# Five small edits to a decoder-layer kernel: gate products in exact parts, a token-major first query block, a root carried in the last sum, squares moved, and four raw weight tiles in another pool

## The chip, the cores and the metric

One core of a Trainium2 chip runs the whole layer in one launch. The metric is the device time of an execution in microseconds; lower is better. Profiles are of one execution each, and their span is somewhat shorter than the device time.

## The reference, cut to what matters

A decoder layer in float32 for one sequence of 256 tokens and width 2048:

```python
hn = rmsnorm(h, norm_mix_w)
q, k, v, g_ret, xr, yr, g_a, g_b = split(hn @ w_in)            # 2048 -> 14336 columns
ret_out = silu(g_ret) * head_groupnorm(chunkwise_retention(rotary(q), rotary(k), v))
xr = causal_dwconv(xr)                                          # 4 taps
gate_r = sigmoid(blockdiag(xr, rg_w_a) + b_a)                   # 16 blocks of 128x128
gate_i = sigmoid(blockdiag(xr, rg_w_x) + b_x)
a = exp(-8 * gate_r * softplus(-lam))
hr = scan(h = a * h + sqrt(1 - a*a) * gate_i * xr)              # over the tokens
rnn_out = gelu(yr) * hr
h = h + (sigmoid(g_a) * (ret_out @ w_proj_ret) + sigmoid(g_b) * (rnn_out @ w_proj_rnn)) @ w_mix_out
h = h + memory_cross_attention(rmsnorm(h), rmsnorm(mem)) @ xa_w_o   # 4 heads of 512, 256 memory tokens
h = h + (silu(gate) * value) @ ffn_w_down                       # gate, value = conv3(rmsnorm(h) @ ffn_w_up)
return rmsnorm(h, final_norm_w)
```

## The kernel before, in words

**Exact parts.** Every large product is made of three TensorE products of `fp32r` parts: a value is split into `hi`, its rounding to `fp32r`, and `lo`, the rest. Products are hi x hi, lo x hi and hi x lo. Only the gates of the recurrence use plain float32 products (`sm<-xr,rgw`, line 214 through `recur`).

**Weights.** All weights come from one packed array in the order of use, in chunks of 512 rows by 512 columns (1 MB; the first chunks are smaller). For each chunk SyncE (SP) issues the load into a `raw` tile (three buffers), ScalarE (ACT) casts `raw` to `hi` (line 276) and VectorE (DVE) subtracts to get `lo` (line 277), both in two halves of 128x1024 with six buffers each, that is, three chunks. A chunk is loaded and split two chunks ahead of its use (`AHEAD`). The first chunk's `hi` casts are done by DVE (line 274).

**A block** is a product of 256 tokens with a matrix of 512 columns: four chunks of 24 TensorE products of 128x512 (5.45 us a chunk in the chain of waits). `steps_n` makes it by token (tokens in the output's partitions: `products_n`, for both halves `tt` of the tokens); `steps_t` makes it by feature, for the first query block alone; `joined` adds the two halves of its accumulators. The first two blocks of the stream, q and v, run alternately, chunk by chunk, with the chunk sizes of `EARLY`.

**Rows to features.** A block by token that is needed by feature is copied to `rows` (lines 407, 409), its 16-bit halves spread to planes `pl` by two ACT copies (line 385), turned by two DMA transposes that SP issues (`pt<-pl`, line 387), and joined to `f` by two ACT copies (line 396) some chunks later.

**Order.** TensorE's products keep program order (`mm`). What belongs between the chunks is queued by `later(n, fn)` and emitted n + 1 chunks later; the other engines' order is then chosen by a scheduler by priority, and each engine's queue runs in that order. Tiles of 4 KB a partition come from one pool of 27 buffers (`big`), others from pools with few buffers each; a tile that takes a buffer waits for the last reader of what lay there.

**The recurrence** is done in four blocks `b` of 512 features. For each: the XR block and the YR block of `w_in`, then the convolution of XR (lines 775, 777), two bursts (`recur`, `pr` = 0 and 1, emitted `RG_WAIT` and `RG_WAIT + 1` chunks later) of four gate products each, followed by tanh (`tr`, `ti`, lines 742 and 743), exp and tanh (`aa`, `tt`), then root and scan; `gelu_y` makes the stationary parts of the next product.

**The residuals** (`residual`, for w_mix_out and xa_w_o) add a block to `hrow[b]`, square it (line 867) for the next norm, and turn it by `by_dma`. The squares of the memory rows (`memory_steps`) run during the second block of w_mix_out.

**The end.** `last_down` makes the last block of the last product in column halves of 256, with squares and sums for the final norm; `part` collects the earlier sums and `rsqrt_small` (lines 509 to 512) multiplies, adds the epsilon and takes the power -1/2 on GpSimd (POOL).

Of the kernel before, what the change touches and what calls it, by code (L numbers as in the profile page):

```python
# [34 lines left out]
WARM = 8  # L35
URGENT = 5
FREE = 300
# [101 lines left out]
def hybrid_layer(  # L139
# [93 lines left out]
    def prefetch(n):  # L233
        while len(ahead) < n and taken[0] < len(stream):
# [5 lines left out]
            at[0] += size  # L240
            raw = wp.tile([P, KC, BW], F32, tag="raw", bufs=RAW_BUFS, name=nm("raw"))
            k2 = row // (KH * P)
# [5 lines left out]
            for a, b in zip(cuts, cuts[1:]):  # L248
# [62 lines left out]

    def steps_t(w, row, st, nk, col):

        accs = [acc(), acc()]
        first = gemms[0] == 0
        phase = 0
        for k0, n, parts in chunks(nk, w, row, col):
            last = k0 + n >= nk
            tiles = [(kk, j) for j in range(2) for kk in range(n)]
            if first and k0 == 0:  # L320
                runs = [[(t, pr, kk, j) for t in (0, 1)] for kk in range(n) for pr in range(2) for j in range(2)]
            elif last:
                runs = [[(t, pr, kk, j) for kk, j in tiles] for pr in range(2) for t in (1 - pr, pr)]
            else:
                runs = [[(t, pr, kk, j) for pr in range(2) for kk, j in tiles] for t in (phase, 1 - phase)]
                phase = 1 - phase
            for i, run in enumerate(runs):
                for t, pr, kk, j in run:
                    k = k0 + kk
                    sx = st[k // 2][:, k % 2, :]  # L330
                    part = parts[kk // KH][t][:, kk % KH, (2 * pr + j) * P : (2 * pr + j + 1) * P]
                    a = accs[pr][:, j, :]
                    if t == 1:
                        a, sx = a[:, S:BW], sx[:, 0:S]
                    mm(
                        a, part, sx, start=k == 0 and t == 0, stop=k == nk - 1 and t == 0, skip_group_check=True
                    )
                if i + 1 == len(runs) // 2 and not last and not first and isinstance(st, Pairs):
                    st[(k0 + n) // 2 + 1]
            yield accs  # L340

    def gemm_t(*args):
        return ended(steps_t(*args))

    def products_n(o, sx, hi, lo, tt, start, stop):
        h = sx[:, tt * P : (tt + 1) * P]
        l = sx[:, S + tt * P : S + (tt + 1) * P]
        mm(o, h, hi, start=start, stop=False)
        mm(o, l, hi, start=False, stop=False)
        mm(o, h, lo, start=False, stop=stop)  # L350

    def steps_n(w, row, st, nk, col):

        a = acc()
        for k0, n, parts in chunks(nk, w, row, col):
            for tt in range(2):
                for kk in range(n):
                    k = k0 + kk
                    hi, lo = (t[:, kk % KH, :] for t in parts[kk // KH])
                    products_n(a[:, tt, :], st[k // 2][:, k % 2, :], hi, lo, tt, k == 0, k == nk - 1)  # L360
                if tt == 0 and isinstance(st, Pairs):
                    st[min(NT, k0 + 3 * n) // 2 - 1]
            yield a

    def gemm_n(*args):
        return ended(steps_n(*args))
# [34 lines left out]
    def turned_rows(a, r, then, wait=1):  # L401
# [8 lines left out]
        by_dma(rows, then, wait)  # L410

    def joined(a, s="j"):

        c = tmp("c")
        o = tmp(s)
        with tc.high_priority(URGENT):
            act.copy(c, a[:, :, S:BW])
            dve.tensor_tensor(out=o, in0=a[:, :, 0:S], in1=c, op=ALU.add)
        return o

# [161 lines left out]

    qjoin = [joined(t, "q") for t in next(q_steps)]
    assert next(q_steps, None) is None
    later(0, tables)
# [86 lines left out]
    for g in range(2):  # L672
        dec = big([P, 4, S], s="dec")
        vs, turned = [], ([], [])
        for b, o in enumerate((O_Q, O_K)):
            if g + b:
                def rotate_both(f, o=turned[b]):
                    o.append(rotated(f[:, 0:2, :]))
                    later(0, lambda: o.append(rotated(f[:, 2:4, :])))
# [8 lines left out]
            if g + b == 0:  # L688
                turned[0].extend(rotated(q) for q in qjoin)
# [42 lines left out]

    def recur(b, rgw, xr, pr, aa, tt_, ti):

        for j in (2 * pr, 2 * pr + 1):
# [28 lines left out]
    for b in range(4):  # L764
        rgw = big([P, 2, 4, P], s="rgw")
        for i, src in enumerate((rg_w_a, rg_w_x)):
            sp.dma_start(out=rgw[:, i], in_=src[0, 4 * b : 4 * b + 4].rearrange("g i j -> i g j"))
        xr = {}

        def conv_x(f, b=b, xr=xr, rgw=rgw):  # L770
            xr[0] = big([P, 4, S], s="xr")
# [9 lines left out]

            three = []

            def both(pr):
                if pr == 0:
                    three.extend(big([P, 4, S], s=n) for n in ("aa", "tt", "ti"))
                recur(b, rgw, xr[0], pr, *three)

# [51 lines left out]
    def residual(w, st, out, wcol, steps=None):  # L840
# [3 lines left out]
        for b in range(4):  # L844
# [166 lines left out]

    def last_down(b0, hid, n, b):
        h = hrow[b]
        accs = [acc(), acc()]
        parts = [p for _, _, ps in chunks(n, "ffn_w_down", b0 * BW, b * BW) for p in ps]
        for tt in range(2):
            for c in range(2):
                cs = slice(c * S, (c + 1) * S)
                for k in range(n):
                    hi, lo = (t[:, k % KH, cs] for t in parts[k // KH])  # L1020
                    products_n(accs[c][:, tt, 0:S], hid[k // 2][:, k % 2, :], hi, lo, tt, k == 0, k == n - 1)
                y = h[:, tt, cs]
                dve.tensor_add(y, y, accs[c][:, tt, 0:S])
                junk = tp.tile([P, S], F32, tag="tr", bufs=2, name=nm("junk"))
                dve.scalar_tensor_tensor(
                    out=junk, in0=y, scalar=1.0, in1=y, op0=ALU.mult, op1=ALU.mult,
                    accum_out=ss3[:, tt, b + c : b + c + 1],
                )
            part = sp_.tile([P, 1], F32, tag="pt3", bufs=2, name=nm("pt3"))
            dve.tensor_reduce(out=part, in_=ss3[:, tt, 0:4], axis=AX.X, op=ALU.add)  # L1030
            dve.tensor_scalar(out=part, in0=part, scalar1=1.0 / D, scalar2=EPS, op0=ALU.mult, op1=ALU.add)
            r = rsqrt_small(ss3[:, tt, 4:5], 1, 1.0 / D, part)
            for c in (1, 0, 3, 2):
                y = hrow[c][:, tt, :]
                if c == 3:
                    dve.scalar_tensor_tensor(
                        out=y, in0=y, scalar=r, in1=wfin[1][:, 1, :], op0=ALU.mult, op1=ALU.mult
                    )
# [69 lines left out]
```

## Time and profile before

| | us |
|---|---|
| runs: median (lowest to highest of 3) | 2016.69 (2016.46 to 2019.35) |
| the profiled execution, device time | 2016.58 |
| its span | 2014.5 |
| PE busy | 1999.1 |
| DVE busy | 1263.5 |
| ACT busy | 1247.8 |
| POOL busy | 7.7 |
| HBM read | 388.46 MB |

The span is the time from the first to the last instruction that the profiler saw; the 2.1 us between span and device time lie around it. "PE" is TensorE's products, "PEld" its loads of stationary operands, which run beside products. In the groups of instructions, "out<-in" names the tiles, followed by the shape, the number of instructions, the busy time and the mean duration in ns; behind the bar comes the idle time of the engine before them and who ended it. In a chain, each line is start, duration (both us), engine, tile and line, followed back from what ended last. In a table of stretches, the columns are the stretch, its length, the busy time and number of instructions of each of PE, PEld, DVE, ACT and POOL, then the clock granted to TensorE (1.00 is full), the share of the DMA engines' time, and GB/s.

### The profile page before, as it was taken

How to read it: one execution, taken by the hardware profiler on the slowest of the kernel's cores; microseconds unless marked ns; L12 is line 12 of the kernel's file. 1: busy time of each engine (PE TensorE's matmuls, PEld its weight loads, DVE VectorE, ACT ScalarE, POOL GpSimd, SP SyncE). 2: the span in 40 equal slices, each digit the busy share in tenths (PEclk: the TensorE clock that was granted, in tenths of full speed). 3: DMA queues.
4: the chain of work that ended last, by engine and by line, in shares of the span. 5: the costliest groups of instructions: out<-in, count | busy, mean ns of one | idle time of the engine just before them, and what ended most of it. 6: DMA issues, size and time to landing. Idle time of an engine off the chain costs nothing.

```text
span 2014.5 us, 23604 instructions
## 1 busy us (share of the span) xinstructions
PE 1999.1 (99%) x9044; PEld 1664.3 (83%) x9044; DVE 1263.5 (63%) x1563; ACT 1247.8 (62%) x1506; POOL 7.7 (0%) x12
## 2 busy tenths in 40 slices
PE   9999999999999999999999999999999999999998
PEld 7888888888888888878888888888888888888887
DVE  5867757888545555456555555566775577664675
ACT  5556648888444455487675656766763466744763
POOL 0000000000000000000000000000000000000000
PEclk9999999999999999999999999999999999999999
DMA  8755757665555566767766645767665566655663
GB/s 299 233 210 172 235 199 196 235 206 188 209 190 192 195 207 211 260 227 241 227 208 205 197 176 184 217 205 215 214 223 216 195 191 217 232 210 200 208 230 125
DMA packets 189376, 423.02 MB, mean 210 GB/s; under 512 B 131664, under 2 KB 136400, under 8 KB 144208
## 3 DMA queue, kind: packets, MB, share of 16 engines
q1 hardware_dynamic: 188832, 421.00, 63.5%
q8 instruction: 70, 1.15, 0.2%
q10 hardware_dynamic: 432, 0.53, 0.1%
q14 instruction: 42, 0.34, 0.0%
HBM read 388.46 MB, written 2.10 MB: 194 GB/s over the span
## 4 chain that ended last, share of the span: by engine, by line
PE 96%; DMA 1%; ACT 1%; issue 1%; DVE 1%; SPq 0%; POOLq 0%; POOL 0%; ACTq 0%; DVEq 0%
PE acc L214 94%; PE sm L214 3%; DMA raw<-in_wall 1%; DMA pt<-pl 1%; DVE lo L277 0%; ACT pl L385 0%; ACT hi L276 0%; ACT f L396 0%; ACT junk L867 0%; DVE nat L852 0%; ACT s L451 0%; SPq L249 0%; ACT nat L1042 0%; DVE s L452 0%; SPq L387 0%
## 5 line engine op out<-in xcount | busy, mean ns | idle before, releaser
L214 PE MATMUL acc<-hi,s 128*128 128x512 f32 (+1 forms) x5680 | 1739.9, 388 | 3.0 <-ACT hi L276 2.5
L277 DVE TENSOR_TENSOR lo<-raw,hi 128x1024 fp32r<-128x1024 f32 (+1 forms) x714 | 859.4, 1218 | 645.9 <-ACT hi L276 629.5
L214 PEld LDWEIGHTS acc<-hi,s 128*128 128x128 f32 x5680 | 1062.4, 188 | 220.1 <-ACT hi L276 2.9
L214 PE MATMUL acc<-lo,s 128*128 128x512 f32 (+1 forms) x2840 | 1100.6, 388 | 0.5 <-DVE lo L277 0.5
L276 ACT CAST hi<-raw 128x1024 fp32r<-128x1024 f32 (+1 forms) x712 | 733.0, 1048 | 497.5 <-PE acc L214 428.1
L214 PEld LDWEIGHTS acc<-lo,s 128*128 128x128 f32 x2840 | 533.7, 188 | 110.1 <-DVE lo L277 1.0
L396 ACT COPY f<-pt 128x1024 uint16<-128x1024 uint16 x118 | 151.4, 1349 | 85.0 <-DMA pt<-pl 85.0
L385 ACT COPY pl<-rows 128x1024 uint16<-128x1024 uint16 x90 | 89.7, 1044 | 64.5 <-DVE rows L409 55.8
L409 DVE TENSOR_SCALAR rows<-acc,ro 128x512 f32<-128x512 f32 x68 | 47.7, 742 | 3.1 <-PE acc L214 3.1
L965 DVE SCALAR_TENSOR_TENSOR fv<-f,pf,fv 128x255 f32<-128x255 f32 (+1 forms) x88 | 35.8, 477 | 0.7 <-ACT fv L963 0.7
L965 DVE SCALAR_TENSOR_TENSOR fg<-f,pf,fg 128x255 f32<-128x255 f32 (+1 forms) x88 | 35.6, 477 | 0.0
L452 DVE SCALAR_TENSOR_TENSOR s<-f,pb,s 128x256 fp32r<-128x256 f32 x48 | 20.1, 478 | 6.6 <-ACT s L451 6.6
L963 ACT ACTIVATE fv<-f,pf 128x256 f32<-128x256 f32 x44 | 22.9, 592 | 0.0
L963 ACT ACTIVATE fg<-f,pf 128x256 f32<-128x256 f32 x44 | 22.8, 591 | 0.0
L428 ACT ACTIVATE s<-fo 128x512 fp32r<-128x512 f32 x22 | 13.6, 633 | 14.2 <-DVE fo L985 14.2
L777 DVE SCALAR_TENSOR_TENSOR xr<-f,pa,xr 128x255 f32<-128x255 f32 (+2 forms) x48 | 19.9, 478 | 3.1 <-ACT xr L775 3.0
L451 ACT ACTIVATE s<-f,pb 128x256 fp32r<-128x256 f32 x48 | 20.6, 498 | 0.0
L385 ACT COPY pl<-nat 128x1024 uint16<-128x1024 uint16 x16 | 15.9, 1042 | 6.9 <-DVE nat L852 6.9
L214 PEld LDWEIGHTS sm<-s,s 128*128 128x128 f32 x144 | 18.8, 191 | 0.9
L214 PE MATMUL sm<-s,s 128*128 128x256 f32 (+1 forms) x144 | 18.6, 279 | 0.0
L214 PE MATMUL acc<-s,hi 128*128 128x512 f32 x64 | 17.4, 410 | 0.4 <-DVE hi L274 0.3
L440 ACT ACTIVATE v<-acc,ro 128x512 fp32r<-128x512 f32 x16 | 10.9, 683 | 7.7 <-DVE v L441 7.7
(152 smaller groups left out, 625.5 us busy)
## 6 DMA issues: line engine op xcount, KB each, us to landing
raw<-in_wall SPq DMA_DIRECT2D x352, 1024.0 KB, 4.8
nat<-in_x SPq DMA_DIRECT2D x8, 512.0 KB, 7.8
raw<-in_wall SPq DMA_DIRECT2D x6, 512.0 KB, 6.8
nat<-in_mem SPq DMA_DIRECT2D x4, 512.0 KB, 9.3
xt<-in_mem_t SPq DMA_DIRECT2D x8, 256.0 KB, 3.6
pt<-pl SPq DMA_TRANSPOSE x118, 4.1
xt<-in_x_t SPq DMA_DIRECT2D x7, 256.0 KB, 8.2
out<-nat SPq DMA_DIRECT2D x6, 256.0 KB, 2.8
```

Source lines behind the costliest of these rows:

```text
L214: tc.keep_in_program_order(pe.matmul(*a, **k))
L276: act.copy(hi[:, ds], raw[:, cs, :])
L277: dve.tensor_tensor(out=lo[:, ds], in0=raw[:, cs, :], in1=hi[:, ds].bitcast(F32), op=ALU.subtract)
L385: act.copy(planes[:, :, h, :], words[:, h])
L396: act.copy(halves_[:, h], turned_[:, h])
L409: dve.tensor_scalar_mul(rows[:, tt, :], a[:, tt, :], r[:, tt : tt + 1])
L428: act.mul(t[:, :, 0:S], src, scale)
L451: act.activation(t[:, j, 0:S], src[:, j, :], AF.Identity, scale=wcol(j))
L452: dve.scalar_tensor_tensor(out=t[:, j, S:BW], in0=src[:, j, :], scalar=wcol(j), in1=t[:, j, 0:S].bitcast(F32), op0=ALU.mult, op1=ALU.subtract,
L777: dve.scalar_tensor_tensor(out=y[:, s:S], in0=z[:, 0 : S - s], scalar=p_cw(3 - s, t), in1=y[:, s:S], op0=ALU.mult, op1=ALU.add,)
L963: act.activation(y, z[:, j, :], AF.Identity, scale=pf[:, 2, t : t + 1], bias=pf[:, 3, t : t + 1])
L965: dve.scalar_tensor_tensor(out=y[:, s:S], in0=z[:, j, 0 : S - s], scalar=pf[:, 2 - s, t : t + 1], in1=y[:, s:S], op0=ALU.mult, op1=ALU.add,)
```

## The change

1. **Gates in exact parts.** The gate weights `rgw` and the convolved XR are each split by `parts_of` into `hi` and `lo` tiles of the big pool (four more tiles for each block), and each float32 gate product becomes three `fp32r` products.
2. **First query block by token.** `steps_t` and `joined` go; the block is made by `steps_n` and takes the way of the other query blocks through `rows`, planes and transposes. In the first chunk the products with `hi` of both token halves come first (`products_n` yields between).
3. **Last sum.** The squares are scaled by 1/D with the sum; the root of what the first columns gave is put into column 513 of `last`, so that the last sum of squares holds all, and the power follows without a multiply and add.
4. **Squares.** In both residuals `by_dma` comes ahead of the squares; the squares of blocks 0 and 1 are emitted two or three steps later, block 1 is joined one step later, and the memory's squares start with the first block, one pair a chunk.
5. **Raw weights.** The first four `raw` tiles come from the big pool; the x rows are loaded from chunk 6 of the stream on (before: 5).

The diff without the removal of `steps_t`, `gemm_t` and `joined`:

```diff
@@ prefetch
-            raw = wp.tile([P, KC, BW], F32, tag="raw", bufs=RAW_BUFS, name=nm("raw"))
+            if i < 4:
+                raw = big([P, KH, BW], s="raw")
+            else:
+                raw = wp.tile([P, KC, BW], F32, tag="raw", bufs=RAW_BUFS, name=nm("raw"))
...
-            if i >= 5:
-                load_x(min(4, i - 4))
+            if i >= 6:
+                load_x(min(4, 2 * i - 11))
@@ products_n
         mm(o, h, hi, start=start, stop=False)
         mm(o, l, hi, start=False, stop=False)
+        yield
         mm(o, h, lo, start=False, stop=stop)
+        yield
@@ steps_n
+            if first and k0 == 0:
                 for kk in range(n):
+                    for _ in zip(*(tile_(tt, kk) for tt in range(2))):
+                        pass
+            else:
+                for tt in range(2):
+                    for kk in range(n):
+                        for _ in tile_(tt, kk):
+                            pass
+                    if tt == 0 and isinstance(st, Pairs):
+                        st[min(NT, k0 + 3 * n) // 2 - 1]
@@
-    q_steps = steps_t("w_in", 0, xs, NT, O_Q)
+    q_steps = steps_n("w_in", 0, xs, NT, O_Q)
...
-    qjoin = [joined(t, "q") for t in next(q_steps)]
-    assert next(q_steps, None) is None
+    q0 = ended(q_steps)
@@ retention blocks
-            if g + b:
-                def rotate_both(f, o=turned[b]):
...
-                turned_rows(gemm_n("w_in", 0, xs, NT, o + g * BW), None, rotate_both, 2 - b)
+            def rotate_both(f, o=turned[b]):
+                o.append(rotated(f[:, 0:2, :]))
+                later(0, lambda: o.append(rotated(f[:, 2:4, :])))
+
+            a = gemm_n("w_in", 0, xs, NT, o + g * BW) if g + b else q0
+            turned_rows(a, None, rotate_both, 2 - b if g + b else 3)
@@ recurrence
+    def parts_of(src):
+
+        hi, lo = (big(list(src.shape), F32R, s="rp") for _ in range(2))
+        act.copy(hi, src)
+        dve.tensor_tensor(out=lo, in0=src, in1=hi.bitcast(F32), op=ALU.subtract)
+        return hi, lo
...
-                mm(gp[:, i, :], rgw[:, i, j, :], xr[:, j, :], start=True, stop=True)
+                product(
+                    gp[:, i, :], [t[:, i, j, :] for t in wparts], [t[:, j, :] for t in xparts], True, True
+                )
...
+        later(3, lambda wparts=wparts, rgw=rgw: wparts.extend(parts_of(rgw)))
...
+            later(RG_WAIT - 2, lambda: xparts.extend(parts_of(xr[0])))
@@ residual
-            squares(h, ss, b)
-            by_dma(hrow[b], lambda f, b=b: turn(f, b, out, wcol))
+            by_dma(h, lambda f, b=b: turn(f, b, out, wcol), 1 + (b == 1))
+            if b < 2:
+                later(2 + b, lambda h=h, b=b: squares(h, ss, b))
+            else:
+                squares(h, ss, b)
@@ memory_steps
-        if b == 1:
+        if b == 0:
             ss = sums()
             for c in range(4):
-                sum_squares(mnat[c], ss, c)
-            rsms.append(rstd_rows(ss))
+                later(c, lambda c=c: sum_squares(mnat[c], ss, c))
+            later(4, lambda: rsms.append(rstd_rows(ss)))
@@ last_down
-                y = h[:, tt, cs]
-                dve.tensor_add(y, y, accs[c][:, tt, 0:S])
+                y = last[:, c * S : (c + 1) * S + c]
+                dve.tensor_add(last[:, cs], h[:, tt, cs], accs[c][:, tt, 0:S])
...
-                    out=junk, in0=y, scalar=1.0, in1=y, op0=ALU.mult, op1=ALU.mult,
+                    out=junk[:, 0 : S + c], in0=y, scalar=1.0 / D if c else 1.0, in1=y, op0=ALU.mult, op1=ALU.mult,
...
-            part = sp_.tile([P, 1], F32, tag="pt3", bufs=2, name=nm("pt3"))
-            dve.tensor_reduce(out=part, in_=ss3[:, tt, 0:4], axis=AX.X, op=ALU.add)
-            dve.tensor_scalar(out=part, in0=part, scalar1=1.0 / D, scalar2=EPS, op0=ALU.mult, op1=ALU.add)
-            r = rsqrt_small(ss3[:, tt, 4:5], 1, 1.0 / D, part)
+                if c == 0:
+                    dve.tensor_reduce(out=before, in_=ss3[:, tt, 0:4], axis=AX.X, op=ALU.add)
+                    dve.tensor_scalar_add(before, before, EPS * D)
+                    pool.tensor_tensor(out=last[:, BW : BW + 1], in0=before, in1=half, op=ALU.pow)
+            r = sp_.tile([P, 1], F32, tag="ro", bufs=5, name=nm("ro"))
+            pool.tensor_tensor(out=r, in0=ss3[:, tt, 4:5], in1=mhalf[:, 0:1], op=ALU.pow)
```

More of the change, by code (lines that the diff above doesn't have):

```diff
@@ L35 @@
 WARM = 8
-URGENT = 5
 FREE = 300
@@ L310, in ended @@
         return a
[L312 to L343, printed above, removed]
     def products_n(o, sx, hi, lo, tt, start, stop):
@@ L349, in products_n, with tile_ @@
         mm(o, l, hi, start=False, stop=False)
+        yield
         mm(o, h, lo, start=False, stop=stop)
+        yield
     def steps_n(w, row, st, nk, col):
         a = acc()
+        first = gemms[0] == 0
         for k0, n, parts in chunks(nk, w, row, col):
-            for tt in range(2):
-                for kk in range(n):
[L358 to L362, printed above, removed]
+            def tile_(tt, kk):
+                k = k0 + kk
+                hi, lo = (t[:, kk % KH, :] for t in parts[kk // KH])
+                return products_n(a[:, tt, :], st[k // 2][:, k % 2, :], hi, lo, tt, k == 0, k == nk - 1)
+            if first and k0 == 0:
+                for kk in range(n):
+                    for _ in zip(*(tile_(tt, kk) for tt in range(2))):
[7 more added lines that the diff above has]
+                        st[min(NT, k0 + 3 * n) // 2 - 1]
             yield a
@@ L410, in turned_rows @@
         by_dma(rows, then, wait)
[L412 to L419, printed above, removed]
     def split_pair(src, scale=None):
@@ L675, in hybrid_layer @@
         for b, o in enumerate((O_Q, O_K)):
-            if g + b:
-                def rotate_both(f, o=turned[b]):
-                    o.append(rotated(f[:, 0:2, :]))
-                    later(0, lambda: o.append(rotated(f[:, 2:4, :])))
-                turned_rows(gemm_n("w_in", 0, xs, NT, o + g * BW), None, rotate_both, 2 - b)
+            def rotate_both(f, o=turned[b]):
[3 more added lines that the diff above has]
+            turned_rows(a, None, rotate_both, 2 - b if g + b else 3)
             if b == 1:
@@ L687, in hybrid_layer @@
             v = gemm_n("w_in", 0, xs, NT, O_V + g * 1024 + b * BW) if g + b else ended(v_steps)
-            if g + b == 0:
-                turned[0].extend(rotated(q) for q in qjoin)
             vs.append(split_rows(v, rs0))
@@ L731, in hybrid_layer, with recur @@
     rnn = []
-    def recur(b, rgw, xr, pr, aa, tt_, ti):
+    def parts_of(src):
[3 more added lines that the diff above has]
+        return hi, lo
+    def recur(b, wparts, xparts, xr, pr, aa, tt_, ti):
         for j in (2 * pr, 2 * pr + 1):
@@ L767, in hybrid_layer, with conv_x @@
             sp.dma_start(out=rgw[:, i], in_=src[0, 4 * b : 4 * b + 4].rearrange("g i j -> i g j"))
-        xr = {}
-        def conv_x(f, b=b, xr=xr, rgw=rgw):
+        xr, wparts = {}, []
+        later(3, lambda wparts=wparts, rgw=rgw: wparts.extend(parts_of(rgw)))
+        def conv_x(f, b=b, xr=xr, wparts=wparts):
             xr[0] = big([P, 4, S], s="xr")
@@ L780, in conv_x @@
                     )
-            three = []
+            three, xparts = [], []
+            later(RG_WAIT - 2, lambda: xparts.extend(parts_of(xr[0])))
             def both(pr):
@@ L786, in both @@
                     three.extend(big([P, 4, S], s=n) for n in ("aa", "tt", "ti"))
-                recur(b, rgw, xr[0], pr, *three)
+                recur(b, wparts, xparts, xr[0], pr, *three)
             for pr in range(2):
@@ L1013, in last_down @@
         h = hrow[b]
+        half = sp_.tile([P, 1], F32, tag="half", bufs=1, name="half")
+        dve.memset(half, 0.5)
         accs = [acc(), acc()]
@@ L1016, in last_down @@
         for tt in range(2):
+            last = big([P, BW + 1], s="last")
+            before = sp_.tile([P, 1], F32, tag="pt3", bufs=2, name=nm("pt3"))
             for c in range(2):
@@ L1020, in last_down @@
                     hi, lo = (t[:, k % KH, cs] for t in parts[k // KH])
-                    products_n(accs[c][:, tt, 0:S], hid[k // 2][:, k % 2, :], hi, lo, tt, k == 0, k == n - 1)
-                y = h[:, tt, cs]
-                dve.tensor_add(y, y, accs[c][:, tt, 0:S])
-                junk = tp.tile([P, S], F32, tag="tr", bufs=2, name=nm("junk"))
+                    for _ in products_n(accs[c][:, tt, 0:S], hid[k // 2][:, k % 2, :], hi, lo, tt, k == 0, k == n - 1):
+                        pass
+                y = last[:, c * S : (c + 1) * S + c]
+                dve.tensor_add(last[:, cs], h[:, tt, cs], accs[c][:, tt, 0:S])
+                junk = tp.tile([P, S + 1], F32, tag="tr", bufs=2, name=nm("junk"))
                 dve.scalar_tensor_tensor(
-                    out=junk, in0=y, scalar=1.0, in1=y, op0=ALU.mult, op1=ALU.mult,
+                    out=junk[:, 0 : S + c], in0=y, scalar=1.0 / D if c else 1.0, in1=y, op0=ALU.mult, op1=ALU.mult,
                     accum_out=ss3[:, tt, b + c : b + c + 1],
                 )
-            part = sp_.tile([P, 1], F32, tag="pt3", bufs=2, name=nm("pt3"))
-            dve.tensor_reduce(out=part, in_=ss3[:, tt, 0:4], axis=AX.X, op=ALU.add)
-            dve.tensor_scalar(out=part, in0=part, scalar1=1.0 / D, scalar2=EPS, op0=ALU.mult, op1=ALU.add)
-            r = rsqrt_small(ss3[:, tt, 4:5], 1, 1.0 / D, part)
+                if c == 0:
[4 more added lines that the diff above has]
+            pool.tensor_tensor(out=r, in0=ss3[:, tt, 4:5], in1=mhalf[:, 0:1], op=ALU.pow)
             for c in (1, 0, 3, 2):
@@ L1036, in last_down @@
                     dve.scalar_tensor_tensor(
-                        out=y, in0=y, scalar=r, in1=wfin[1][:, 1, :], op0=ALU.mult, op1=ALU.mult
+                        out=y, in0=last[:, 0:BW], scalar=r, in1=wfin[1][:, 1, :], op0=ALU.mult, op1=ALU.mult
                     )
```

## The prediction

> **What bounds the kernel now.** First the page's busy times and its chain of waits, then the costliest groups:
>
> ```profile
> PE 1999.1 (99%) x9044; PEld 1664.3 (83%) x9044; DVE 1263.5 (63%) x1563; ACT 1247.8 (62%) x1506; POOL 7.7 (0%) x12
> PE 96%; DMA 1%; ACT 1%; issue 1%; DVE 1%; SPq 0%; POOLq 0%; POOL 0%; ACTq 0%; DVEq 0%
> L276 ACT CAST hi<-raw 128x1024 fp32r<-128x1024 f32 (+1 forms) x712 | 733.0, 1048 | 497.5 <-PE acc L214 428.1
> ```
>
> TensorE is busy 99% of the span, so an edit counts only through PE's own work, PE's stalls and the clock. The last line matters later: ACT stood 428.1 us at a `hi` cast until PE had finished with the cast's buffer (six buffers, three chunks). Whatever stands behind such a cast in ACT's queue waits too; its ACT time is free only if PE doesn't need it.
>
> The chain of the first 52 us and of 860 to 890 us shows both real holes; the stretches show the clock.
>
> ```profile
> 10.13 7.76 DMA raw<-in_wall
> 18.19 0.87 DVE s L452 x2
> 19.07 1.16 DVE lo L277
> 20.27 29.16 PE acc L214 x142
> ```
>
> ```profile
> 876.48 1.88 ACT pl L385 x2
> 878.77 0.61 ACT junk L867 x2
> 879.38 0.94 ACT hi L276
> 881.63 8.58 PE acc L214 x30
> ```
>
> ```profile
> 14.00:18.00 4.00, 3.34 (x17) 2.51 (x16) 1.58 (x3) 1.94 (x4) 0.00 (x0) 1.00 1.02 405
> 22.00:25.00 3.00, 3.00 (x12) 2.53 (x11) 1.74 (x3) 0.91 (x2) 0.00 (x0) 0.56 1.01 395
> 882.00:885.00 3.00, 3.00 (x8) 2.30 (x8) 2.98 (x3) 3.00 (x4) 0.00 (x0) 0.54 0.40 108
> ```
>
> In the stretches the number after POOL's is the granted clock. At 10.13 a weight transfer took 7.76 us; PE then stood 1.15 and 1.61 us and ran at half clock from 21.2 to 24.6. At 880 a `hi` cast came after `pl` copies and squares; PE stood 2.64 us, then ran at half clock from 881.4 to 884.8. Products start every 0.228 us otherwise, 0.427 at half clock, so a half-clock episode of 3.41 us costs 1.7 us. The other holes: three of 0.41 to 0.44 at 5 to 8 us, 0.64 at 1304. Neither group was followed by a slow clock: 1.26 us idle within 2.3 us is too little, 2.76 within 3.1 is enough.
>
> **Start.** Four raw tiles move to the 27-buffer pool, so transfers 4 and 5 no longer wait for a raw buffer; the x loads go one chunk back in SP's queue, but all four are still issued by stream chunk 8, whose squares read the first two. At the 400 GB/s of the stretch the fifth chunk's weights land at 13 to 15 us instead of 15.9 to 17.9: the stalls at 18 to 20 and the half clock go. My replay: chunk 0 ends 0.4 earlier (both token halves use `hi` before `lo`), chunk 2 waits 0.65 for its `lo`, chunk 5 starts at about 23.0 instead of 27.27. That is 4.2. The q block by token runs at 5.44 a chunk against 5.54 to 5.56 for three chunks: 0.3. Against it, the block now goes through `rows` (2 x 0.68, DVE), `pl` (2 x 1.04, ACT), two transposes on SP and `f` (2 x 1.34), where a copy (0.59) and an add (0.69) for each half stood; in DVE's order both `rows` stand ahead of the second `lo` of the next chunk: 0.6 late. Net 3.9; bounds 2 (transfers as slow as the 7.76 above half the time) and 4.8.
>
> **Gates.** Eight bursts of four F32 products:
>
> ```profile
> 341.73 1.73 PE sm L214 x8
> 343.45 5.45 PE acc L214 x24
> 348.90 1.73 PE sm L214 x8
> 350.63 38.09 PE acc L214 x168
> ```
>
> Afterwards a burst is 12 fp32r products of 128x256. In the attention a 128x256 fp32r product starts every 0.1195 us, so 1.43 instead of 1.73: 0.30 x 8 = 2.4 gained. Each block adds two casts (1.05, ACT) and two subtractions (1.22, DVE). The time is there (ACT 8.8 to 10 of each 10 us busy around 340 to 360, about 7 around 390 to 440), the place is not always. Read from the compiled order of the changed kernel, with these durations, T being PE's end of the chunk before the burst:
> - Block 1, first burst. ACT has `hi`, `hi`, then the split of xr. The second `hi` reuses the buffer of the chunk that ends at T. So: `hi` until T+1.1, split `hi` until T+2.1, subtraction on DVE until T+3.35, and PE's second product needs that. Stall 3.3.
> - Blocks 1 and 2, second burst. Its PSUM tile is free when the two tanh `ti` of the first burst are done, but these stand behind a `hi` that waits for T: 0.1 + 0.95 + 0.36 = 1.4, then two activations and a `ti` for the second tile: 0.7 more. Stall 2.1 each.
> - Block 3. A tile of the recurrence takes the slot of a gate weight part, so ACT waits for the second burst; the gelu rows then come 9 us late, and the last recurrent stationary is ready at 516.3, where PE wants it at 514.2. Stall 2.1 (0 to 3).
> - Block 0 and the other bursts: the split stands behind a `hi` whose buffer is free one chunk earlier; nothing.
> Sum 9.6, bounds 5 and 12. What is queued behind (casts) is two chunks ahead and is late only with PE.
>
> Does the clock fall after them? In the 3.3 stall PE is idle 2.15 and 1.25 us with one product between, more than the 2.76 in 3.1 that sufficed: one episode, 1.7. The 2.1 stalls hold 1.4 to 2.1 us idle, between the 1.26 that wasn't enough and 2.76: bounds 0 and 1.7 each; I take 0, the nearer row. [...]
>
> **Squares spread.** In the residual after w_mix_out, `by_dma` goes ahead of the squares, squares of blocks 0 and 1 come two to three chunks later, block 1 is joined a chunk later and the memory squares (0.52 to 0.62 each) lie in an ACT gap at 843 to 850 where ACT waited for a transpose. In the new ACT order the `hi` casts that came at 879.4 follow one `pl` pair and one square, at about 867, their raw having landed at 861.8. The 880 stall and its half clock go: 2.64 + 0.11 + 0.69 + 0.36 + 7 x 0.20 = 5.2, of which I take 5.0; SP gets the transposes 1.2 earlier, ahead of a weight load that isn't due for two chunks; POOL gets the memory's pow two blocks earlier and has nothing else (7.7 us busy in all). Bounds 2.6 (half of it returns elsewhere in those 40 us, where my margins are 3.7 us at least) and 5.2. At xa_w_o the order is as before: the 0.64 at 1304 stays.
>
> **Last sum.** The tail loses one TENSOR_SCALAR, 0.21 and its gap: 0.25. The added POOL pow (0.55) lies between the two column halves, with more than 2.5 us of products to hide it; without them it would cost 0.55.
>
> **Sum.** 3.9 + 2.4 + 5.0 + 0.25 = 11.55 gained; 9.6 + 1.7 = 11.3 lost. The profiled execution took 2016.58 (span 2014.5, 2.1 around it), 0.11 under the median of the runs: 2016.58 - 0.25 = 2016.3. About 0.2%, 4.0 us, is what a measurement of this kernel can tell from no change: under 2012.7 is faster, over 2020.7 slower.
>
> **Rivals.**
> 1. *The stalls are not there* or mostly not: the split and the tanh come in time because an earlier lag of PE gives ACT its lead. For: a lead of 10 us in casts nearly everywhere. Against: a `hi` cast cannot lead PE by more than its six buffers, and the group row above shows ACT standing there. All hidden: 2016.58 - 11.55 = 2005.0; half of them: 2010. [...] Chance 0.3.
> 2. *Slower: half clock after all four stalls.* [...] Price 3 x 1.7 = 5.1: 2021.4. It decides from two episodes on top (2019.7 + any other loss). Chance 0.2.
> 3. *The start doesn't gain:* four more tiles give SP its issues sooner, but the DMA moved only 180 to 340 GB/s before 14 us; if chunk 4 lands as before, the 1.15 and 1.61 stalls stay with their clock: 2.0 instead of 0, so gain 0 to 1, time 2019 to 2020. Chance 0.1, and with another loss it is slower.
> 4. *The squares don't repair 880* because the casts still stand behind a late transpose: 2021.3. Chance 0.1.
> The forecast itself 0.3, its own range 2012.7 to 2020.
>
> Range: from half the stalls hidden and a good start (2007) to all half clocks and a little more (2022.5). Faster 0.30 (rival 1); same 0.38 (forecast, most of rival 3); slower 0.32 (rivals 2 and 4, the rest of 3).
>
> **What would show it.** In the changed profile: chain of the first 30 us without the `lo` wait at 19 and clock 1.0 throughout; `sm` bursts of 1.43; PE idle before `sm` products at about 384 (3.3, waiting for DVE L708) and at 392 and 440 (2.1, waiting for ACT `ti`), half clock after the first; PE waiting for DVE `s` near 510; no gap at 880; end of the last product to end of span 7.5 instead of 7.7. The prediction is wrong if `sm` waits for nothing (then near 2005) or if three or four half-clock stretches lie between 380 and 520 (then above 2020).

## The result and the profile after

The changed kernel takes 2025.45 us (median of six runs, 2024.33 to 2027.84) against 2016.76 for the kernel before: ratio 1.0044, 95% interval 1.0033 to 1.0054. It is slower by 9 us, outside the range of the prediction. The profiled execution took 2025.38, its span 2023.6, 9.1 more than before's 2014.5.

From the page of the changed kernel: its busy times, its chain and the group of the gate products (columns as before):

```profile
PE 2001.8 (99%) x9044; PEld 1663.5 (82%) x9044; DVE 1271.5 (63%) x1570; ACT 1258.6 (62%) x1516; POOL 8.8 (0%) x14
...
PE 78%; ACT 1%; DMA 1%; DVE 0%; issue 0%; POOLq 0%; POOL 0%; ACTq 0%; DVEq 0%; SPq 0%
...
L213 PE MATMUL sm<-rp,rp 128*128 128x256 f32 x96 | 15.6, 310 | 8.0 <-ACT ti L723 3.4
```

The busy shares hardly move. (The chain could be followed back only to 390 us, so its shares add up to 80%.) The gate products, which waited for nothing before, now have 8.0 us of idle time ahead of them. What PE waited for over the whole span (total, times, longest; all in us):

```profile
PE sm L213 <- ACT ti L723: 3.4, 4, 1.3
PE sm L213 <- ACT rp L707: 2.8, 1, 2.8
PE acc L213 <- DVE s L425: 2.0, 2, 1.3
PE sm L213 <- DVE rp L708: 1.9, 1, 1.9
PE acc L213 <- DVE s L402: 1.1, 1, 1.1
```

The stretches that answer to those shown of before, and those of recurrence block 1:

```profile
14.00:18.00 4.00, 4.00 (x19) 3.30 (x18) 3.93 (x6) 3.40 (x5) 0.00 (x0) 1.00 1.04 415
...
22.00:25.00 3.00, 3.00 (x15) 2.49 (x14) 1.93 (x3) 3.00 (x5) 0.00 (x0) 1.00 1.07 406
878.00:885.00 7.00, 7.00 (x32) 5.82 (x31) 4.72 (x4) 5.91 (x11) 0.00 (x0) 1.00 1.00 273
384.00:391.00 7.00, 2.31 (x10) 1.58 (x9) 7.00 (x12) 2.69 (x3) 0.00 (x0) 0.90 0.27 94
391.00:397.00 6.00, 6.00 (x21) 5.11 (x21) 1.56 (x2) 2.83 (x4) 0.00 (x0) 0.55 0.69 249
...
403.00:407.00 4.00, 4.00 (x15) 3.31 (x14) 2.58 (x5) 4.00 (x11) 0.00 (x0) 0.57 0.68 262
```

The first three are whole: no wait, clock 1.00. In 384 to 391 PE worked 2.31 of 7 us while DVE worked all of them; ACT was busy for 2.69. Then the clock is halved twice.

Where the time went is seen by setting each accumulating product of one trace against the same product of the other, counted from the end (times are those of before's trace; the numbers are us that the changed kernel's profiled execution loses, or gains where negative, in each part):

| part | forecast | measured |
|---|---|---|
| start, to 55 us | -3.9 | -3.07 |
| block 0's bursts | -0.6 | -0.56 |
| block 1 (two bursts, half clock) | +6.5 | +11.23 |
| block 2 | +1.5 | +1.82 |
| block 3 and the late stationary | +1.5 | +1.96 |
| 880 to 894 | -5.0 | -5.07 |
| 922 to 937 | 0 | +1.71 |
| to 1309 and on | 0 | +1.20 |
| after the last product | -0.25 | -0.14 |
| sum | -0.25 | +9.08 |

### The profile page after: what moved, and what is told of

The parts are those of the page before. It is cut to its first block, busy times and chain, and to the rows that moved or that the text cites. A ratio compares the mean times of both kernels' runs of the same rounds, so it can differ in the third digit from the quotient of the medians.

```text
span 2023.6 us, 23642 instructions
## 1 busy us (share of the span) xinstructions
PE 2001.8 (99%) x9044; PEld 1663.5 (82%) x9044; DVE 1271.5 (63%) x1570; ACT 1258.6 (62%) x1516; POOL 8.8 (0%) x14
## 4 chain that ended last, share of the span: by engine, by line
PE 78%; ACT 1%; DMA 1%; DVE 0%; issue 0%; POOLq 0%; POOL 0%; ACTq 0%; DVEq 0%; SPq 0%
PE acc L213 76%; PE sm L213 2%; DMA pt<-pl 0%; ACT hi L278 0%; DMA raw<-in_wall 0%; ACT f L378 0%; ACT tt L725 0%; DVE lo L279 0%; ACT aa L724 0%; DVE xr L740 0%; ACT ti L723 0%; ACT nat L1035 0%; ACT L737 0%; DVE ti L738 0%; ACT tt L737 0%
## 5 line engine op out<-in xcount | busy, mean ns | idle before, releaser
L213 PE MATMUL acc<-hi,s 128*128 128x512 f32 (+1 forms) x5744 | 1761.5, 388 | 4.4 <-DVE s L425 2.0
L213 PEld LDWEIGHTS acc<-hi,s 128*128 128x128 f32 x5744 | 1075.3, 188 | 226.8 <-DVE s L425 2.7
L213 PE MATMUL acc<-lo,s 128*128 128x512 f32 (+1 forms) x2872 | 1113.7, 388 | 0.7 <-DVE lo L279 0.7
L213 PEld LDWEIGHTS acc<-lo,s 128*128 128x128 f32 x2872 | 540.2, 188 | 112.3 <-DVE lo L279 2.0
L213 PE MATMUL sm<-rp,rp 128*128 128x256 f32 x96 | 15.6, 310 | 8.0 <-ACT ti L723 3.4
L213 PEld LDWEIGHTS sm<-rp,rp 128*128 128x128 f32 x96 | 13.7, 208 | 10.7 <-ACT ti L723 4.6
```

The lines of the kernel that those rows point to most:

```text
L213: tc.keep_in_program_order(pe.matmul(*a, **k))
```

## The experiments

Every ratio is against the kernel before, run on the same chip; 0.001 is 2 us. "Ahead" and "behind" are by the product-by-product comparison of the profiled execution with that of before.

**1. Each part alone, and the gates taken out.**

`no_gates`, the changed kernel with

```diff
-                product(
-                    gp[:, i, :], [t[:, i, j, :] for t in wparts], [t[:, j, :] for t in xparts], True, True
-                )
+                mm(gp[:, i, :], rgw[:, i, j, :], xr[:, j, :], start=True, stop=True)
```

and `parts_of` gone:

> The changed kernel with the gates as float32 products again; all else of the change stays. Theory A (the gates' casts and subtractions, in queues that run in order, are what costs: from the traces the stretch 341 to 519 us went from 3.1 to 11.4 us behind): that goes, and 2011 to 2013 is left, with at most about 1 us of wait at the first burst of block 1, since ACT and DVE finish the convolution at 386 whether PE is early or not. Theory B (the earlier start uses up ACT's and DVE's lead, so that PE waits in block 1 with any gates): 2016 to 2018, with 3 us or more of wait there. Theory C (slots of the big pool, raw tiles in it): no better than 2020.

Measured: 2014.71, ratio 0.9985 (0.9976 to 0.9993). From 55 to 880 us it stays 3.17 ahead; PE waits for nothing between. What PE waits for in its whole span begins

```profile
PE acc L213 <- ACT s L424: 2.2, 1, 2.2
PE acc L213 <- DVE lo L279: 1.5, 5, 0.5
PE acc L213 <- DVE s L425: 1.1, 1, 1.1
```

No `sm` product is among them. The early start is kept through the recurrence: theory B falls. The time is above theory A's 2011 to 2013 because of a new wait at 922 us (below).

`gates_only`, the kernel before with the gates' edit alone:

> The kernel before with the gates as three products of exact parts and nothing else. ACT's order in the recurrence is the same as in the changed kernel. Theory A: 2016.7 - 2.4 for the products + waits of 3.3, 2.1, 2.1 and 2.1 + one half-clock episode of 1.7 = 2025.6, 2023 to 2029. Theory B: PE comes 3.6 us later to block 1 than in the changed kernel, so most of the waits vanish: 2015 to 2019.

Measured: 2035.74, ratio 1.0084 (1.0071 to 1.0097): the gates cost all of the loss and more. The profiled execution took 2028.84, with the same waits as the changed kernel (first burst of block 1 2.72 + 2.16) and one half-clock stretch behind them (granted clock 0.96 from 384 to 391, 0.77 from 391 to 397). Its time lies in theory A's 2023 to 2029, the median 7 us above it. Theory B was hardly tested here: the start of this execution was 2.06 ahead of before's, so PE came to the burst at 385.9, only 1 us later than in the changed kernel. The other runs are 6 to 7.5 longer, most of them with a mean granted clock of 0.994 or 0.995 where the profiled one has 0.998, so more half clock is a likely part of the difference (0.003 of 2030 us is 6); those runs have no trace.

`sq_only`, the squares' edits alone, and `start_tail`, the start and the last sum alone:

> The kernel before with the squares of both residuals and of the memory moved, and nothing else. The wait at 880 us and its half clock go: -5.1. If the new waits of the changed kernel at 934 us (1.55) and 1312 us (1.2 more than before) come from this part, 2014.3; if they come from other parts, 2011.6.

> The kernel before with the first query block by token, the four raw tiles in the big pool and the last sum; gates and squares as before. 3.1 + 0.1 gained by 55 us. Theory A: 2013.5 to 2014.5, about 1 us going at the first burst of block 1. Theory B: all 3 us are waited away in block 1: 2016 to 2017.

Measured: 2013.46, ratio 0.9986 (0.9977 to 0.9995), and 2012.81, ratio 0.9979 (0.997 to 0.9988). Both parts gain; `sq_only` lies between its two expectations. In its trace the 880 us wait is gone (-5.07), but 2.0 come back at 921 to 923: that new wait comes with the squares. In `start_tail` 3.05 are kept from 55 to 880 us.

`raw_only`, of the start only

```diff
+            if i < 4:
+                raw = big([P, KH, BW], s="raw")
...
+            if i >= 6:
+                load_x(min(4, 2 * i - 11))
```

> The kernel before with the first four raw tiles in the big pool and the x rows loaded one chunk later, and nothing else; the first query block stays by feature. If the raw tiles are what removes the two waits and the half clock at 18 to 25 us: most of the start's 3 us, with the 880 us wait staying: 2013 to 2014.5. If the order of the products by token does it: 2016 or more.

Measured: 2013.4, ratio 0.9988 (0.9979 to 0.9997); by 55 us it is 3.37 ahead, against 3.05 with the whole start part (`start_tail`). These are single executions, and those with the whole start part spread from 2.3 to 3.8. The raw tiles, with the later x rows, carry the start's gain; of the first query block by token nothing is seen beyond that spread.

**2. Why the gates cost: place, amount or slots.**

`g_late` and `g_late_prio`:

```diff
-                later(RG_WAIT + pr, lambda pr=pr: both(pr))
+                later(RG_WAIT + (b in (1, 2)) + pr, lambda pr=pr: both(pr))
```

and, in the second, `with tc.high_priority(FREE):` around `parts_of`'s two instructions and the tanh of `tr` and `ti`.

> The changed kernel with the two gate bursts of recurrence blocks 1 and 2 emitted one chunk (5.45 us) later; the work is the same. Theory A (place): in the changed kernel the split of xr for block 1 is complete at 390.1 us, 5.4 us after PE came to the first burst; a chunk later PE comes at 390.2, so the first burst's 5.1 us wait and its half clock (3.4) go; the second bursts keep theirs (2.0 each), since ACT still has two casts ahead of the tanh: 2025.5 - 8.5 = 2017, 2015 to 2019. Theory D (amount: ACT and DVE have too much to do in this stretch, so a wait only moves): 2022 or more.

> As g_late, and with a higher priority for the parts of the gates and for the two tanh that free the gates' PSUM tiles, so that in ACT's order they come ahead of casts that wait for PE. Theory A: the waits at both bursts go, and with the products' 2.4 gained the recurrence costs no more than the 2 us of late stationary at its end: 2009 to 2013. Theory D: 2018 or more.

Measured: 2024.36 (1.0047, 1.0034 to 1.0059) and 2025.36 (1.0053, 1.0039 to 1.0067). My theory of the place alone falls. In `g_late` the first burst's wait of block 1 did go (3.4 ahead from 405 to 436 us, where the changed kernel is 7.6 behind), but 2.1 then came at block 2's first burst, 2.0 at its second, and 5.5 at block 3's first, with half clock behind that one (0.62 from 490 to 495; 1.00 from 430 to 475). In `g_late_prio` no wait for `ti` is left; PE waits 5.4 and 1.7 for the parts of block 3, and 3.5 for a weight subtraction at 415 us. Two stretches of `g_late`, ahead of those bursts:

```profile
435.00:441.00 6.00, 4.12 (x22) 3.24 (x22) 6.00 (x9) 3.19 (x4) 0.00 (x0) 1.00 0.32 90
483.00:490.00 7.00, 1.89 (x8) 1.52 (x8) 7.00 (x12) 2.07 (x3) 0.00 (x0) 0.79 0.37 125
```

DVE is busy without a gap (6.00 of 6, 7.00 of 7) while PE stands, as it was at block 1 in the changed kernel. The wait moves to later blocks.

`g_unused` makes the parts but multiplies in float32; `g_held` does too, and POOL reads a column of each part together with the result of the burst, so that the slots stay taken; `g_held_bp29` and `bp29` (the changed kernel itself) have 29 buffers, the two `sig` tiles coming from the big pool; `no_gates_bp29` is the control.

```diff
+                recur(b, rgw, xr[0], pr, *three)          # g_unused
+                for t in (*wparts, *xparts):              # g_held, besides
...
+                    pool.tensor_tensor(
+                        out=held, in0=flat[:, 0:1].bitcast(F32), in1=three[0][:, 2 * pr + 1, 0:1], op=ALU.add
+                    )
...
-    bp = ctx.enter_context(tc.tile_pool(name="bp", bufs=27))
+    bp = ctx.enter_context(tc.tile_pool(name="bp", bufs=29))
```

> The changed kernel with the gates' parts made but not read: the products are float32 as before, so the casts and subtractions take their places in ACT's and DVE's queues without PE waiting for them. Theory A in its narrow form (PE waits for the parts): all waits go, 2025.5 - 14.4 + 0.6 = 2011 to 2013. In its wide form (the added work moves other work of the queues, the tanh and the last stationary): the first burst's wait falls from 5.1 to 2, the second's 2.0 stays, the late stationary stays: 2018 to 2021. Theory D: 2021 or more.

> As g_unused (parts made, products float32), but each part is read in one column by POOL together with what ACT makes after a burst, so that its slot of the big pool stays taken until the second burst is done, as in the changed kernel; PE still waits for no part. If the slots are what costs: near the changed kernel, 2022 or more. If PE's wait for the parts is: near g_unused's 2017.8, 2016 to 2019.5.

> As g_held, with 29 instead of 27 buffers in the big pool (the room comes from the two sigmoid tiles of the later merge, which move into the big pool). PE waits for no part; only the taken slots differ. If the slots are what g_held loses against g_unused (7.5 us): at least half comes back, 2018 to 2021. If not: 2024 or more.

> The changed kernel with 29 instead of 27 buffers in the big pool, else as it is. ACT's order around the bursts of blocks 1 and 2 is the same as in the changed kernel, so their waits (5.1, 2.0, 2.0 and half clock) stay if the place in the queue makes them: 2022 to 2025, with only the late stationary of 2 us at the recurrence's end better. If the slots make them: 2016 to 2020.

> The control: float32 gates and the rest of the change, with 29 buffers. If 27 are enough without the gates' parts: 2014.7 as with 27, within 2. If slots were short already there: 2010 to 2012.

The last column is from one profiled execution each, the median from all runs.

| kernel | median us | ratio (95%) | lost from 341 to 519 us |
|---|---|---|---|
| no_gates | 2014.71 | 0.9985 (0.9976 to 0.9993) | 0 |
| no_gates_bp29 | 2013.18 | 0.9990 (0.9981 to 0.9999) | 0 |
| g_unused | 2017.84 | 1.0013 (1.0004 to 1.0021) | 5.25 |
| g_held_bp29 | 2020.74 | 1.0025 (1.0015 to 1.0036) | 8.1 |
| g_held | 2025.32 | 1.0044 (1.0032 to 1.0057) | 14.0 |
| the changed kernel | 2025.45 | 1.0044 (1.0033 to 1.0054) | 14.45 |
| bp29 | 2023.86 | 1.0041 (1.0027 to 1.0054) | 14.75 |

The casts and subtractions alone, read by nobody, cost 0.0028, 5.6 us, mainly by the second burst of block 1, where PE waits for `ti`, which stands in ACT's order behind a `pl` pair (that waits for `rows`) and two weight casts:

```profile
PE sm L213 <- ACT ti L721: 3.3, 2, 3.1
```

That is the wide form of the theory (place and amount): the added work displaces other work. Holding the slots as well costs 6 us more by the medians, without PE waiting for any part. In the profiled executions it is 8.75: 2.9 at block 1's second burst, with half clock there (seven of its products took 3.35 us from 396.9, the first burst's eight 1.73; the mean granted clock is 0.995, in `g_unused` 0.998), and 5.85 from 497 us on. In the chain of `g_held` one sees the slot: ACT's join of block 3's gelu rows starts when POOL has read the part:

```profile
502.41 0.75 POOL held L771
503.16 0.02 issue
503.18 2.57 ACT f L378 x2
505.75 0.02 issue
505.77 1.28 ACT L735
```

7.3 us are lost between 497 and 519 there; with two more buffers 2.2, and the time falls by 0.0019, as the slot theory expected. But in the changed kernel itself two more buffers change nothing that can be measured (1.0041 against 1.0044), as the expectation for places said; of the late stationary at the end of the recurrence, 2.3 us in the changed kernel's trace, 1.4 are left. There the parts are late at block 1 before any slot is short. So slots are a cost of this edit that appears when the first one is taken away, and not what makes the changed kernel slow. With the float32 gates 27 buffers are enough.

`g_pool`, `g_pool_late`, `g_pool_bp29`: the parts made by POOL.

```diff
-        act.copy(hi, src)
-        dve.tensor_tensor(out=lo, in0=src, in1=hi.bitcast(F32), op=ALU.subtract)
+        pool.tensor_copy(hi, src)
+        pool.tensor_tensor(out=lo, in0=src, in1=hi.bitcast(F32), op=ALU.subtract)
```

The second has block 1's bursts a chunk later, the third 29 buffers.

> The changed kernel with the parts of the gates made by POOL, which is idle there, instead of ACT and DVE: the slots, the products and PE's wait for the parts stay, ACT's and DVE's added work goes. How long POOL takes for a 128x1024 copy and subtraction no trace has shown; for block 1 the convolution ends at about 386 us and PE comes at 384.7. If the places in ACT's and DVE's queues are what costs: a wait of 3 to 8 us and its half clock at block 1's first burst, little at blocks 2 and 3: 2015 to 2021. If the slots cost: 2022 or more.

> As g_pool, and block 1's two bursts one chunk (5.45 us) later, so that PE comes at 390 us. If the places in ACT's and DVE's queues are what costs, little is left of the waits in the recurrence and the 2.4 us of the products are kept: 2010 to 2015. If ACT and DVE are too full there with any gates, or the slots cost: 2018 or more.

> The gates' parts made by POOL (1.9 us a copy and 2.4 a subtraction in the trace) and 29 buffers: both costs eased at once. PE's waits for POOL's parts (2.3 at block 1) stay. If the amount on ACT and DVE and the slots are the two causes: 2015 to 2019. If PE's wait for the parts is the main cause: 2021 or more.

Measured: 2022.7 (1.0028, 1.0019 to 1.0037), 2025.96 (1.0044, 1.0031 to 1.0058), 2023.19 (1.0035, 1.0023 to 1.0048). With ACT's and DVE's added work gone 0.0016 comes back, a quarter of the gates' 0.0059 (1.0044 - 0.9985), and the waits of the second bursts go (the four of `ti` are one of 0.4). 2022.7 lies where its expectation had put the slots, but with 29 buffers it gets no better, which by `g_pool_bp29`'s expectation leaves PE's wait for the parts. Most of what is left is indeed waiting for POOL, whose two steps are longer (duration in ns: least, median, most):

```profile
L707 POOL CAST rp<-xr x3: 1902/1903/1904, 382.5 to 479.6; 128x1024 fp32r<-128x1024 f32 x3
L708 POOL TENSOR_TENSOR rp<-xr,rp x3: 2345/2362/2381, 384.5 to 481.5; 128x1024 fp32r<-128x1024 f32 x3
```

and PE waits 4.9 in three places for L708. Later bursts failed again (expected 2010 to 2015): the convolution of block 2 ended at 436, where PE had come at 432, and PE stood 6.5 us with half clock behind it (the burst's products took 415 ns from 438.3 on, in `g_pool` 283). So whoever makes the parts, PE comes to a first burst shortly before or after the convolution has ended, and a cast and a subtraction in a row (2.3 us on ACT and DVE, 4.3 on POOL) lie between. That the gates' parts cause the loss is shown by `no_gates`. That this path and the displaced work cause it together, and not one alone, is argued from these runs; no run took DVE's work alone away, so how much is DVE's full stretch stays open.

**3. The wait at 922 to 937 us.**

`no_gates_ls` makes the logits' scale on POOL alone; `ls_early` also loads the memory's transposed rows a block earlier:

```diff
-    dve.tensor_scalar_mul(lscale, rstd_rows(ss1), float(XD**-0.5))
+    pool.tensor_tensor(out=half_sums, in0=ss1[:, :, 0:2], in1=ss1[:, :, 2:4], op=ALU.add)
...
-        if b == 3:
+        if b == 2:
             ms.load(2)
             for k2 in range(4):
-                later(k2, lambda k2=k2: ms[k2])
+                later(k2 + 2, lambda k2=k2: ms[k2])
```

In `sq_only` the chain at this place is

```profile
917.97 0.72 ACT junk L870 x3
...
918.71 0.17 DVE var L503
...
919.15 0.71 POOL ro L512
...
919.89 0.07 DVE lscale L890
...
921.14 0.30 DVE lo L277
...
922.27 0.49 DVE s L452
...
922.81 1.20 PE acc L214 x4
```

DVE stands at a sum of squares and at POOL's power, with weight subtractions behind it.

> The changed kernel with float32 gates, and the scale of the attention's logits made from the four sums on POOL instead of DVE and POOL. Theory E (the new wait at 922 us comes because DVE's queue holds a sum of the last block's squares, and the power on POOL after it, ahead of a weight subtraction): the 2.3 + 1.6 us of wait there and the half clock (3.4) go against the 2014.7 of the kernel with float32 gates: 2008 to 2011. Theory F (the subtraction itself comes late because stationary splits stand ahead of it): 1 to 2 us at most, 2013.

> As no_gates_ls, with the loads and splits of the memory's transposed rows begun one block (four chunks) earlier. In no_gates_ls six such loads go to the DMA queue between 897 and 900 us, ahead of two weight loads that land 7.5 and 9.5 us later, and PE waits 1.4 + 1.2 us at 920. If these loads and splits are the rest of that wait: 2012.0 - 2.6 = 2009.5, 2008 to 2011. If it is the squares and the sum of the last block: no change, 2012.

Measured: 2012.05 (0.9982, 0.9974 to 0.9991): 1.4 + 1.2 us of wait are left of 2.3 + 1.6 and the half clock is gone (mean granted clock 0.999, in `no_gates` 0.997); that lies between theories E and F, and against `no_gates` the intervals overlap. Then 2008.43 (0.9958, 0.9945 to 0.9970): of the wait 0.4 us is left. The rest was the memory's loads and splits. `ls_early` beats both kernels: by 0.4% the one before, and by 17 us the changed one.

## Why the prediction was wrong

**Right in mechanism and size:** the second bursts of blocks 1 and 2 (1.98 and 2.03 us measured for 2.1), block 3 with the late stationary (+1.96 for +1.5; ACT's `tt` waits for the second burst until 500.6, and the gelu rows are joined at 505.0 instead of 487.0, 9 us more than PE's own delay), the products' own gain (0.28 a burst for 0.30), the wait at 880 (5.07 for 5.0). These are 2 to 5 us pieces in 2000, which is why the page's shares say so little. The size at 880 was in part luck: some 1.5 of it is the half clock behind the wait (0.54 from 882 to 885 before). The traces of `gates_only`, `start_tail` and `raw_only` keep the old squares and the wait, and are 1.1 to 1.8 us better there than before; in `start_tail` the clock was 1.00 from 880 to 884.

**The step that failed first:** "T+3.35" for block 1's first burst. It took ACT's second `hi` for what the split of xr waits for. That cast did end at T+1.0, but the split then still waited for the convolution. Here is the changed kernel's timeline without the other instructions (start and duration in us, engine, operation; in brackets how long the engine had stood and what ended it):

```profile
381.90 4.81 DVE L758 SCALAR_TENSOR_TENSOR xr<-f,pa,xr 128x255 f32<-128x255 f32 x12
...
384.90 1.04 ACT L278 CAST hi<-raw 128x1024 fp32r<-128x1024 f32 x1 [0.30 <-PE acc L213]
386.63 2.35 DVE L279 TENSOR_TENSOR lo<-raw,hi 128x1024 fp32r<-128x1024 f32 x2
386.79 1.04 ACT L707 CAST rp<-xr 128x1024 fp32r<-128x1024 f32 x1 [0.84 <-DVE xr L758]
387.89 0.38 PE L213 MATMUL sm<-rp,rp 128*128 128x256 f32 x1 [2.80 <-ACT rp L707]
388.90 1.21 DVE L708 TENSOR_TENSOR rp<-xr,rp 128x1024 fp32r<-128x1024 f32 x1
...
390.17 2.71 PE L213 MATMUL sm<-rp,rp 128*128 128x256 f32 x11 [1.89 <-DVE rp L708]
```

PE was there at 384.9; the convolution (12 instructions of DVE, 4.8 us) ended at 386.7, the cast began at 386.8, and DVE had two weight subtractions (from 386.6 to 388.9) ahead of the rest of xr, which began at 388.9. So the subtraction ended at T+5.2 instead of T+3.35, and PE lost, counted from when each product was due, 2.96 + 2.16 = 5.1 instead of 3.3. Before, PE came at 388.6, after a convolution that had ended at 386.2; I let the 3.6 us by which PE was early take PE to the burst sooner, and did not ask whether xr was there.

**The term mis-sized most:** the half clock. Forecast one stretch of 3.41 us, 1.7; measured 6.83 us from 389.5 (PE still stood in the first 0.6 of it) and 3.41 from 403.2. Block 1's 11.23 less its waits (5.1 and 2.0) and with the products' own gain (0.56) added leaves 4.7 for them. Rival 2 (half clock behind the other waits) was right for block 1's second burst, with 2.0 us idle, and not for block 2's with the same idle time; so of the bounds 0 and 1.7 each came true once, and taking 0 was wrong for block 1. At block 1's second burst 2.0 us idle in pieces of 1.4 and 0.5 was followed by half clock (0.50 from 403.2 to 406.6), at block 2's, in pieces of 1.5 and 0.5, by none (1.00 from 445 to 480).

**Rival 1 (the waits are not there)** is refuted by the changed kernel's waits. **Rival 3 (no gain at the start)** too: clock 1.00 from 14 to 25 us. The start fell 0.8 short in this pair, by waits of 1.5 us between 10 and 14 and by PE's being at half clock until 7.3 (products 0.43 us apart up to there, 0.23 from 7.6 on); and the start of before is not the same in each execution: `gates_only` and `sq_only`, with the same start, were 2.06 and 0.52 ahead of before's at 55 us, so 3 may be more than the part gives on the average.

**Rival 4 (880 not repaired)** is refuted, but its sign was right 40 us further on: I looked at margins only up to where the old wait had been, and the moved splits and the sum ahead of `lo` took 1.71 back at 922 to 937 in the changed kernel, and 6.4 in the profiled execution of `no_gates`, where the clock fell as well (0.82 from 918 to 922, 0.55 from 922 to 928). All traces with the moved squares but `ls_early`'s lose 1.5 to 6.4 there, those with the old ones 0.2 to 0.8. The prediction put nothing there.

**1304 and on:** the prediction took the order at xa_w_o for unchanged, though the squares move in both residuals. The 1.20 lost there can't be put down to that: over all traces this place lies between -0.8 and +1.2 against before's, and between -0.8 and +0.7 with the old squares. Its cause stays open.

**Why the range missed:** 0.3 was given to the waits' being hidden, and that reached down to 2007; the upper end, 2022.5, took the half clocks of rival 2 and little else, where the first burst (+1.8), the half clock (+3.0) and 934 and 1312 us (+2.9) came together.

## What to carry to other kernels

A cheaper product needs its operands earlier: ask what the last producer ends at now, and whether two more steps fit between it and the consumer; 2.2 us of PE's time (8 x 0.28) were bought here with a cast and a subtraction, 2.3 us, on a path that at block 1 had 2.4 us to spare before the change (from 386.2 to 388.6). When PE gets earlier by one part of a change, replay the other parts with PE early. And follow a queue beyond the repaired wait, until its margins are what they were.

## What the runs showed that I had not expected

Waits of the same length were not followed by the same clock. In the changed kernel PE stood 1.44 + 0.53 us (from when each product was due) at block 1's second burst, and the clock was 0.50 from 403.2 to 406.6. At block 2's second burst it stood 1.50 + 0.53, and the clock was 1.00 from 445 to 480. From 523 to 527 PE worked 2.48 of 4.00 us, and the clock was 1.00 there and from 527 to 531.

Nor did the wait at 880 do the same in each execution: in before's PE worked 2.99 of the 6.00 us from 876 to 882 and the clock was 0.50 from 881.4 to 884.8; in `start_tail`'s it worked 1.93 of the 4.00 us from 876 to 880 and the clock was 1.00 from 880 to 884. So the same wait brought some 1.5 us of half clock on top in one execution and none in another. What makes the difference these figures don't show.

The half clock also lasted differently long: 6.83 us from 389.5 behind the first burst's wait of block 1, though PE was idle in only 0.6 us of it, and 3.41 behind the second burst's; in `gates_only`, behind 2.72 + 2.16 us of wait, some 3.3 (from 0.96 over 384 to 391 and 0.77 over 391 to 397).

POOL makes a 128x1024 copy of xr to `fp32r` in 1.9 us and the subtraction in 2.36 (`g_pool`), against 1.05 on ACT and 1.21 on DVE (the changed kernel).
